# A two-layer encoder trunk on one Trainium2 core: the second layer starts with another product, and its first activations are made one half of the tokens at a time

## The chip, the cores and the metric

The kernel runs on one core of a Trainium2 chip. The metric is device time in microseconds (us) for the whole program, two layers from input to output. The engines are named as in the profile: PE (matrix multiplies; PEld is its weight load), DVE (vector), ACT (scalar), POOL (GpSimd), SP (which only issues transfers here). Each engine takes its instructions from a queue of its own in the order in which the program was built, and waits on semaphores for the others.

## What is computed

Two equal layers over 256 tokens of 2048 channels. Of a layer, cut to what matters here:

```python
h = rms_norm(x, norm_pre) * (1 + scale) + shift          # per-channel scale and shift
proj = h @ w_in                                          # all input products share h
rq, rk, rv, rg, lx, lg, mq, mkv, mkr, mg, merge_logits = split(proj)
y_ret, y_lru, y_mla = retention(rq, rk, rv, rg), rglru(lx, lg), mla(mq, mkv, mkr, mg)
merged = sum of sigmoid(merge_logits[b]) * (y_b @ w_branch[b])  over the three branches
y = merged @ w_out
x = x + (1 + res_gate) * rms_norm(y, norm_post)
```

The h of the second layer therefore needs the x of the first, and that needs the row sums of squares of y: two norms stand between the last product of layer one and the first product of layer two.

## The kernel before

**Tiles.** Tokens lie in two halves of 128 (hf 0 and 1), channels in 16 d-tiles of 128 (kt 0 to 15). Products are made in fp32r from split operands: a weight tile is cast to a high part `wh` on ACT (L308) and the rest `wl` is subtracted on DVE (L309), 128x1024 each; the activations are kept as pairs of a high and a low part in the same way. Each product is high*high + high*low + low*high, so three matmuls per step.

**Three forms of product.** `gemm_x` (L349) has the tokens as the stationary operand: a step is one d-tile and one half of the tokens, six matmuls of 512 columns. `gemm_w` (L377) has the weights stationary and 256 tokens moving: 384 matmuls of 256 columns for a product of 1024 output columns. `gemm_pair` (L396) also has the weights stationary, but moves high and low part in one matmul of 512 columns and adds one of 256: 128 of each. `run` (L978) chooses: lx, lg, mg, rq and rk are of the second kind, and they go through `gemm_pair` unless something has to be called between their steps (`before`), in which case they go through `gemm_w`.

**The end of layer one.** The last part of the product with `w_out` (L1190 to L1193) is sorted by half, so the bank of half 0 is complete some 5 us before that of half 1. Then the closing chain (L1205 to L1256), whose order on ACT, DVE and POOL is written out by hand: `close(hf)` squares the last quarter of y on ACT, weighs it on DVE (L1188) and makes 1/rms(y); `add(hf, k)` makes a quarter of the new x (L1224; one quarter, `ASIDE`, on POOL in L1221 and L1222); `sq` squares it on ACT (L477); `bias` and `rstd` make 1/rms(x).

**The start of layer two.** `h_chain` (L1068) multiplies x by 1/rms for both halves (L600, L603), then `h_tiles` (L605) turns the d-tiles on PE (L614, into a small PSUM bank `mi`), applies scale and shift (L617, DVE) and splits the result (L625 on ACT, L626 on DVE). The first three calls make d-tiles 0, 1 and 2 to 3; the others make two d-tiles each, ahead of the product that uses them. `hold` keeps the second half of the first weight load behind those first calls. The order of the products is `first` (L994): lx, lg, mqkv (the latents of the attention branch), mg and two merge logits. Since lx must call `h_chain` between its steps, it goes through `gemm_w`.

**What sets the order.** PE and SP run in the order in which the code is written. On the other engines a scheduler places instructions by priority; what is written by hand, or under `tc.high_priority(offset=LATE)`, stands ahead of the rest. Between ACT and DVE the framework lets only one at a time read a PSUM tile: an instruction that reads it waits until the other engine's read is over.

Of the kernel before, what the change touches and what calls it, by code (L numbers as in the profile page):

```python
# [19 lines left out]
P = 128  # L20
# [11 lines left out]
ASIDE = [((0, 3),), ((0, 3), (1, 0))]  # L32
# [22 lines left out]
def hybrid_trunk(ctx: ExitStack, tc: tile.TileContext, a, out):  # L55
# [293 lines left out]
    def gemm_x(act, w, r0, c0, kts, banks, ncol=W1, before=None, late=False):  # L349
# [3 lines left out]
        parts = [[k] for k in range(kts[0], kts[1], step)]  # L353
        if late:
            parts[-2:] = [parts[-2] + parts[-1]]
        for part in parts:
            steps, spare = [], []
            for k0 in part:
                nk = min(step, kts[1] - k0)
                if before is not None:  # L360
                    before(k0)
                pieces = load_split(wsrc(w, r0, k0, nk, c0, ncol), nk, ncol, spare if k0 > part[0] else None)
# [69 lines left out]
    def group(act, w, c0, mode, kts, res, func, partial, before):  # L432

        banks = [bank() for _ in range(4)]
        if mode == "x":
            drive(gemm_x(act, w, 0, c0, kts, [banks[0:2], banks[2:4]], before=before))
# [168 lines left out]
    def h_tiles(l, xs, act, k0, k1):  # L605
# [14 lines left out]
        return last  # L620

# [343 lines left out]
    def layer(l, xs, r):  # L965
        w_in = a["w_in"][l]
        H = Act(NKT)
# [10 lines left out]
        def run(n, kts=(0, NKT), partial=None, before=None):  # L978
# [7 lines left out]
            r = group(H, w_in, c0, m, kts, part.get(n), func, partial, before)  # L986
# [7 lines left out]
        first = ["lx", "lg", "mqkv", "mg", ("lru", 0), ("lru", 1)]  # L994
        lat = [None]
# [68 lines left out]
        else:  # L1064
            xn = [two() for _ in range(2)]
            done_k = [0]

            def h_chain():  # L1068
                with tc.high_priority(offset=LATE):
                    for c0 in (0, 2 * P):  # L1070
                        normed(xs, xn, r, c0, c0 + 2 * P, True)
                    for k in (0, 1):
                        h_tiles(l, xn, H, k, k + 1)
                    last = h_tiles(l, xn, H, 2, 4)
                hold.extend(last)
                for k in range(0, NKT, 2):
                    if k >= 4 and k % 4 == 0:
# [4 lines left out]
                    if k > 2:  # L1082
                        h_tiles(l, xn, H, k, k + 2)
# [5 lines left out]
            def ahead(k0):  # L1089
                while done_k[0] < min(NKT, k0 + 4):  # L1090
                    named["h"].step()

            for n in first:
                run(n, before=ahead if n == first[0] else None)
# [229 lines left out]
```

## Time and profile before

| | |
|---|---|
| median of 3 runs | 1984.01 us (1981.05 to 1984.06) |
| the profiled execution | 1987.14 us, of which the span from first to last instruction is 1985.4 us |
| PE busy | 1896.3 us, 96% of the span |
| DVE busy | 1427.9 us, 72% |
| ACT busy | 993.5 us, 50% |
| mean granted TensorE clock | 0.992 of full |

Matmuls are pipelined, so a busy PE is not PE at its peak: what tells is the distance from one start to the next and the time in which PE has nothing to do. The 40 slices of the page have PE at 9 tenths and over in all but four: the first, the third, the last, and the one from 993 to 1042 us, in which layer one ends.

### The profile page before, as it was taken

What the parts mean: (1) busy time and instruction counts of PE and PEld (TensorE: products, weight loads), DVE (VectorE), ACT (ScalarE), POOL (GpSimd) and SP (SyncE); (2) the same over time, 40 slices, a digit from 0 to 9 for tenths busy, and PEclk for the clock granted to TensorE, in tenths of its full rate; (3) what the DMA queues carried; (4) which work ended last, traced back from release to release, by engine and by line L of the source; (5) the groups of instructions that cost most, each with busy time, mean ns of one, the idle gap of its engine ahead of it and who ended that gap; (6) DMA issues with size and microseconds to landing.
All of it is one profiled execution on the core that took longest, in us unless ns stands there. A gap on an engine that the chain in (4) does not pass through costs nothing.

```text
span 1985.4 us, 25224 instructions
## 1 busy us (share of the span) xinstructions
PE 1896.3 (96%) x9884; PEld 1618.8 (82%) x9884; DVE 1427.9 (72%) x1832; ACT 993.5 (50%) x1301; POOL 187.4 (9%) x140
## 2 busy tenths in 40 slices
PE   1969999999999999999989999999999999999998
PEld 1868889778888888888879888888898888888786
DVE  7899989888877778877556765446575447886555
ACT  4744547834444445444454775444445444544443
POOL 2233411100000010101110010000000001010110
PEclk9989999999999999999999999999999999999999
DMA  8778774587877678878665555555554556878663
GB/s 261 281 270 297 270 260 154 203 282 269 264 257 271 236 275 271 279 286 279 214 219 185 170 170 191 197 195 179 184 189 149 200 196 219 271 274 285 219 213 127
DMA packets 169335, 457.06 MB, mean 230 GB/s; under 512 B 12224, under 2 KB 20432, under 8 KB 169216
## 3 DMA queue, kind: packets, MB, share of 16 engines
q1 hardware_dynamic: 165536, 443.44, 65.1%
q0 software_dynamic: 3536, 11.75, 1.9%
q8 instruction: 77, 1.26, 0.2%
q14 instruction: 42, 0.34, 0.0%
q10 hardware_dynamic: 144, 0.26, 0.0%
HBM read 451.23 MB, written 4.19 MB: 229 GB/s over the span
## 4 chain that ended last, share of the span: by engine, by line
PE 80%; DVE 11%; DMA 4%; ACT 2%; issue 2%; POOL 0%; DVEq 0%; ACTq 0%; POOLq 0%
PE acc L373 54%; PE acc L405 8%; DVE wl L309 4%; PE acc L406 4%; DVE slot L512 3%; PE acc L392 2%; PE acc L393 2%; PE acc L391 2%; DMA raw<-in_w_in 1%; DVE slot L446 1%; ACT wh L308 1%; DMA raw<-in_w_branch 1%; DMA raw<-in_mla_w_ukv 1%; DMA raw<-in_ada_w 1%; PE mi L858 1%
## 5 line engine op out<-in xcount | busy, mean ns | idle before, releaser
L309 DVE TENSOR_TENSOR wl<-raw,wh 128x1024 fp32r<-128x1024 f32 (+1 forms) x636 | 796.5, 1255 | 452.8 <-ACT wh L308 450.4
L308 ACT CAST wh<-raw 128x1024 fp32r<-128x1024 f32 (+1 forms) x636 | 662.4, 1045 | 790.9 <-PE acc L373 493.4
L373 PE MATMUL acc<-wh,pair 128*128 128x512 f32 x3552 | 990.7, 393 | 4.2 <-DVE slot L446 3.8
L373 PEld LDWEIGHTS acc<-wh,pair 128*128 128x128 f32 x3552 | 661.7, 188 | 145.1 <-DVE slot L446 7.3
L373 PE MATMUL acc<-wl,pair 128*128 128x512 f32 x1776 | 558.6, 391 | 6.6 <-DVE wl L309 6.6
L373 PEld LDWEIGHTS acc<-wl,pair 128*128 128x128 f32 x1776 | 332.5, 188 | 80.7 <-DVE wl L309 11.2
L405 PE MATMUL acc<-pair,wh 128*128 128x512 f32 x768 | 273.3, 400 | 1.0 <-DVE slot L419 1.0
L512 DVE SCALAR_TENSOR_TENSOR slot<-raw,c_act,slot 128x512 f32<-128x512 f32 (+1 forms) x326 | 255.8, 786 | 6.1 <-DMA raw<-in_ada_w 1.7
L406 PE MATMUL acc<-pair,wl 128*128 128x256 f32 x768 | 215.9, 281 | 1.8 <-DVE wl L309 1.7
L405 PEld LDWEIGHTS acc<-pair,wh 128*128 128x128 f32 x768 | 144.3, 188 | 35.8 <-DVE slot L419 1.3
L391 PE MATMUL acc<-pair,wh 128*128 128x256 f32 x512 | 148.9, 291 | 5.0 <-ACT pair L625 5.0
L392 PE MATMUL acc<-pair,wh 128*128 128x256 f32 x512 | 147.8, 289 | 0.8 <-DVE pair L626 0.8
L393 PE MATMUL acc<-pair,wl 128*128 128x256 f32 x512 | 147.8, 289 | 0.3 <-DVE wl L309 0.3
L406 PEld LDWEIGHTS acc<-pair,wl 128*128 128x128 f32 x768 | 145.1, 189 | 2.9 <-DVE wl L309 2.7
L391 PEld LDWEIGHTS acc<-pair,wh 128*128 128x128 f32 x512 | 101.2, 198 | 6.1 <-ACT pair L625 5.8
L392 PEld LDWEIGHTS acc<-pair,wh 128*128 128x128 f32 x512 | 101.1, 197 | 1.7 <-DVE pair L626 1.4
L393 PEld LDWEIGHTS acc<-pair,wl 128*128 128x128 f32 x512 | 100.9, 197 | 0.8 <-DVE wl L309 0.7
L507 POOL TENSOR_TENSOR slot<-slot,slot 128x512 f32<-128x512 f32 (+1 forms) x49 | 76.0, 1552 | 106.3 <-ACT slot L503 101.1
L1113 POOL TENSOR_TENSOR slot<-slot,slot 128x512 f32<-128x512 f32 x32 | 50.7, 1599 | 252.4 <-DVE slot L1110 252.4
L446 DVE TENSOR_TENSOR slot<-acc,slot 128x512 f32<-128x512 f32 x96 | 62.4, 680 | 2.3 <-PE acc L393 1.4
L850 POOL DMA_DIRECT2D slot<-in_ret_gn x4 | 2.3, 569 | 593.0 <-PE mi L802 362.6
L503 ACT ACTIVATE slot<-raw,c_act 128x512 f32<-128x512 f32 (+1 forms) x64 | 40.0, 662 | 28.3 <-DMA raw<-in_ada_w 28.0
(241 smaller groups left out, 1373.5 us busy)
## 6 DMA issues: line engine op xcount, KB each, us to landing
raw<-in_w_in SPq DMA_DIRECT2D x224, 1024.0 KB, 5.0
raw<-in_ada_w SPq DMA_DIRECT2D x96, 1024.0 KB, 6.7
raw<-in_w_branch SPq DMA_DIRECT2D x48, 1024.0 KB, 6.3
raw<-in_w_out SPq DMA_DIRECT2D x32, 1024.0 KB, 5.4
raw<-in_mla_w_ukv SPq DMA_DIRECT2D x8, 1024.0 KB, 5.9
raw<-in_mla_w_uq SPq DMA_DIRECT2D x8, 768.0 KB, 4.5
slot<-in_x SPq DMA_DIRECT2D x8, 512.0 KB, 8.8
slot<-in_k_decay POOLq DMA_DIRECT2D x4, 512.0 KB, 5.1
```

Source lines behind the costliest of these rows:

```text
L308: nc.scalar.copy(wh, raw[:, c0:c0 + n])
L309: sub = nc.vector.tensor_tensor(out=wl, in0=raw[:, c0:c0 + n], in1=wh.bitcast(F32), op=ALU.subtract)
L373: mm(b[:, 0:w_n], x, ws[:, j * w_n:(j + 1) * w_n], start=st, stop=sp)
L391: mm(dst, wh[:, cs], act.H(kt), start=first, stop=False, skip_group_check=True)
L392: mm(dst, wh[:, cs], act.L(kt), start=False, stop=False, skip_group_check=True)
L393: mm(dst, wl[:, cs], act.H(kt), start=False, stop=last, skip_group_check=True)
L405: mm(v3(b, T), wh[:, cs], act.both(kt), start=kt == 0, stop=False)
L406: mm(b[:, 0:T], wl[:, cs], act.H(kt), start=False, stop=kt == NKT - 1)
L446: nc.vector.tensor_tensor(out=dst, in0=b, in1=dst, op=ALU.add)
L507: nc.gpsimd.tensor_tensor(out=acc[1], in0=acc[1], in1=t, op=ALU.add)
L512: nc.vector.scalar_tensor_tensor(acc[0], src, c, acc[0], ALU.mult, ALU.add)
L1113: nc.gpsimd.tensor_tensor(out=dst, in0=dst, in1=gate[hf][:, cs], op=ALU.add)
```

## The change

1. **Order.** In layer two the order of the products starts with mqkv, then lx and lg. mqkv goes through `gemm_x` and now calls the h chain between its steps; lx goes through `gemm_pair`.
2. **First steps of mqkv.** `gemm_x` takes an argument `soon`. With it the first weight load (d-tiles 0 and 1) and a second one of half the size (d-tile 2) form one part, sorted by half: three steps of half 0, then three of half 1. `soon()` is called ahead of the first step of half 1 and ahead of the second. A load of d-tile 3 alone follows, then pairs as before.
3. **First d-tiles by halves.** A new function `h_half` makes d-tiles 0 to 3 of one half: four transposes into one bank, then for each d-tile one ACT instruction that applies scale and shift and casts to the high part, one DVE instruction that applies scale and shift in full precision, and for each two d-tiles one subtraction.
4. **Closing chain.** In layer one it is ordered by half: all of half 0 up to its 1/rms and the scaled first 512 columns (`begin`), then `close(1)`, one quarter of half 1, `h_half` of half 0, the other three quarters of half 1, and its 1/rms. No quarter goes to POOL. In layer two (the last) nothing moves.

```diff
-ASIDE = [((0, 3),), ((0, 3), (1, 0))]
+ASIDE = [(), ((0, 3), (1, 0))]
...
-        parts = [[k] for k in range(kts[0], kts[1], step)]
+        parts = [[(k, min(step, kts[1] - k))] for k in range(kts[0], kts[1], step)]
+        if soon is not None:
+            parts[:2] = [[(0, 2), (2, 1)], [(3, 1)]]
...
-            if part is parts[-1]:
+            opening = soon is not None and part is parts[0]
+            if part is parts[-1] or opening:
                 steps.sort(key=lambda s: s[1])
-            for kt, hf, (wh, wl) in steps:
+            for i, (kt, hf, (wh, wl)) in enumerate(steps):
+                if opening and i in (3, 4):
+                    soon()
...
+    def h_half(l, xn, act, hf):
+        b, t = mbank(), half_slot()
+        for k in range(4):
+            nc.tensor.transpose(b[:, k * P:(k + 1) * P], xn[hf][0][:, k * P:(k + 1) * P], ident)
+        h, lo = [v3(p, T)[:, :, hf * P:(hf + 1) * P] for p in act.piece(0)]
+        for k in range(4):
+            ks, g, s = slice(k * P, (k + 1) * P), gvec[l][:, k:k + 1], svec[l][:, k:k + 1]
+            i0 = nc.scalar.activation(out=h[:, k, :], in_=b[:, ks], func=AF.Identity, scale=g, bias=s)
+            nc.vector.tensor_scalar(t[:, ks], b[:, ks], g, s, ALU.mult, ALU.add)
+            if k % 2:
+                i1 = nc.vector.tensor_tensor(out=lo[:, k - 1:k + 1, :], in0=v3(t, P)[:, k - 1:k + 1, :], in1=h[:, k - 1:k + 1, :].bitcast(F32), op=ALU.subtract)
...
+        if l:
+            first[:3] = ["mqkv", "lx", "lg"]
...
+                    last = h_half(l, xn, H, 1)
+                yield 1
+                for k in range(4, NKT, 2):
...
+                for k in range(4):
+                    add(0, k)
+                    sq(0, k)
+                bias(0)
+                rstd(0)
+                begin(0)
+                close(1)
+                add(1, 0)
+                sq(1, 0)
+                hold.extend(h_half(l + 1, xn, Hn, 0))
+                for k in (1, 2, 3):
+                    add(1, k)
+                    sq(1, k)
+                bias(1)
+                rstd(1)
+                begin(1)
```

What the built programs show at three places follows; `_NNNN` numbers single tiles, `xss_1248` holds the sums of squares of half 1, `xss_1247` those of half 0, `mi` is the small PSUM bank, `pair_102` holds the first d-tiles of h, slots 79 and 82 hold the new x of half 1, slots 90 and 96 that of half 0 and half 1 times 1/rms, and what a row waits for stands in brackets.

ACT before, from the square root of half 0, behind the first square of half 1, to the first scaled columns of d-tiles 4 and up (L602):

```order
L458 ACTIVATE rstd_1259_8475<-xss_1247_8440,mean_8459 128x1
L477 ACTIVATE junk_8478,xss_1248_8441<-slot_79 128x512 [waits DVE_49,Activation_49]
L477 ACTIVATE junk_8481,xss_1248_8441<-slot_82 128x512 [waits DVE_49,Activation_49]
L477 ACTIVATE junk_8486,xss_1248_8441<-slot_82 128x512 [waits DVE_49,Activation_49]
L458 ACTIVATE rstd_1264_8488<-xss_1248_8441,mean_8483 128x1 [waits DVE_49,Activation_49]
L625 CAST pair_102<-slot_86 128x256 [waits DVE_49]
L625 CAST pair_102<-slot_87 128x256 [waits DMASW1_49,DVE_49]
L625 CAST pair_102<-slot_85 128x512 [waits DVE_49]
L308 CAST wh_8533<-raw_8527 128x1024
L308 CAST wh_8598<-raw_8596 128x1024 [waits DMAHW6_49]
L308 CAST wh_8602<-raw_8596 128x1024 [waits PE_49]
L602 ACTIVATE slot_90<-slot_81,rstd_1259_8475 128x512
```

Both square roots of x and the three casts of h come ahead of any weight cast. ACT now, from behind the same square to the scaled columns (L607):

```order
L635 ACTIVATE pair_102<-mi_8476,svec_136,gvec_135 128x128 [waits PE_49]
L635 ACTIVATE pair_102<-mi_8476,svec_136,gvec_135 128x128 [waits DVE_49] x3
L308 CAST wh_8524<-raw_8518 128x1024
L308 CAST wh_8530<-raw_8528 128x1024 [waits DMAHW6_49]
L482 ACTIVATE junk_8492,xss_1248_8441<-slot_79 128x512 [waits DVE_49,Activation_49]
L482 ACTIVATE junk_8495,xss_1248_8441<-slot_82 128x512 [waits DVE_49,Activation_49]
L482 ACTIVATE junk_8498,xss_1248_8441<-slot_82 128x512 [waits DVE_49,Activation_49]
L463 ACTIVATE rstd_1265_8503<-xss_1248_8441,mean_8500 128x1 [waits DVE_49,Activation_49]
L635 ACTIVATE pair_102<-mi_8552,svec_136,gvec_135 128x128 [waits PE_49]
L635 ACTIVATE pair_102<-mi_8552,svec_136,gvec_135 128x128 [waits DVE_49] x3
L308 CAST wh_8607<-raw_8605 128x1024 [waits DMAHW7_49,PE_49]
L607 ACTIVATE slot_90<-slot_81,rstd_1256_8463 128x512
```

Two weight casts (`wh_8524` and `wh_8530`, d-tiles 1 and 2) have moved in between the first square of half 1 and its other three, and the cast for d-tile 3 (`wh_8607`), which waits for PE, stands ahead of the scaled columns of d-tiles 4 to 7.

DVE before, from the reciprocal of half 1 to the first subtraction for a weight tile after it:

```order
L459 RECIPROCAL rstd_1264_8488<-rstd_1264_8488 128x1 [waits Activation_49]
L603 TENSOR_SCALAR slot_96<-slot_79,rstd_1264_8488 128x256 [waits DVE_49]
L603 TENSOR_SCALAR slot_96<-slot_79,rstd_1264_8488 128x256
L617 TENSOR_SCALAR slot_86<-mi_8506,gvec_135,svec_136 128x256 [waits PE_49,Pool_49]
L617 TENSOR_SCALAR slot_87<-mi_8512,gvec_135,svec_136 128x256 [waits PE_49]
L626 TENSOR_TENSOR pair_102<-slot_86,pair_102 128x256 [waits Activation_49]
L617 TENSOR_SCALAR slot_85<-mi_8518,gvec_135,svec_136 128x256 [waits PE_49,Pool_49]
L626 TENSOR_TENSOR pair_102<-slot_87,pair_102 128x256 [waits Activation_49]
L617 TENSOR_SCALAR slot_85<-mi_8518,gvec_135,svec_136 128x256
L626 TENSOR_TENSOR pair_102<-slot_85,pair_102 128x512 [waits Activation_49]
L603 TENSOR_SCALAR slot_96<-slot_79,rstd_1264_8488 128x512
L309 TENSOR_TENSOR wl_8534<-raw_8527,wh_8533 128x1024 [waits Activation_49]
```

Ahead of these rows the quarters of half 1, its mean and its reciprocal follow each other with no weight tile among them. DVE now, from the last instructions of the first d-tiles of half 0 to the multiplication that starts half 1:

```order
L636 TENSOR_SCALAR slot_86<-mi_8476,gvec_135,svec_136 128x128 [waits Activation_49] x2
L638 TENSOR_TENSOR pair_102<-slot_86,pair_102 128x2x128 [waits DVE_49]
L1242 SCALAR_TENSOR_TENSOR slot_79<-slot_79,rstd_1258_8470,slot_91 128x512
L1242 SCALAR_TENSOR_TENSOR slot_82<-slot_82,rstd_1258_8470,slot_94 128x512 x2
L309 TENSOR_TENSOR wl_8525<-raw_8518,wh_8524 128x1024 [waits Activation_49]
L470 TENSOR_REDUCE mean_8500<-xss_1248_8441 128x1 [waits Activation_49]
L309 TENSOR_TENSOR wl_8531<-raw_8528,wh_8530 128x1024 [waits DMAHW6_49]
L471 TENSOR_SCALAR mean_8500<-mean_8500 128x1 [waits DVE_49]
L464 RECIPROCAL rstd_1265_8503<-rstd_1265_8503 128x1 [waits Activation_49]
L1257 TENSOR_SCALAR slot_96<-slot_79,rstd_1265_8503 128x512 [waits DVE_49]
```

Two weight subtractions (L309) now stand between the quarters of half 1 and its reciprocal, and the three later quarters stand behind the whole of `h_half` of half 0.

PE before, from the end of the product with `w_out` to the first matmuls of lx:

```order
L373 MATMUL acc_8305<-pair_103,pair_101 128x512 x6
L614 MATMUL mi_8506<-ident,slot_90 128x128
L614 MATMUL mi_8506<-ident,slot_96 128x128
L614 MATMUL mi_8512<-ident,slot_90 128x128
L614 MATMUL mi_8512<-ident,slot_96 128x128
L614 MATMUL mi_8518<-ident,slot_90 128x128
L614 MATMUL mi_8518<-ident,slot_96 128x128
L614 MATMUL mi_8518<-ident,slot_90 128x128
L614 MATMUL mi_8518<-ident,slot_96 128x128
L391 MATMUL acc_8498<-pair_102,wh_8529 128x256
L392 MATMUL acc_8498<-pair_102,wh_8529 128x256
L393 MATMUL acc_8498<-pair_102,wl_8530 128x256
```

All transposes of d-tiles 0 to 3, both halves, stand ahead of the first matmul. PE now, behind the 18 matmuls of half 0, from the transposes of half 1 to those of d-tiles 4 and 5:

```order
L631 MATMUL mi_8552<-ident,slot_96 128x128 x4
L378 MATMUL acc_8516<-wh_8520,pair_102 128x512
L378 MATMUL acc_8517<-wh_8520,pair_102 128x512
L378 MATMUL acc_8516<-wl_8521,pair_102 128x512
L378 MATMUL acc_8517<-wl_8521,pair_102 128x512
L378 MATMUL acc_8516<-wh_8520,pair_102 128x512
L378 MATMUL acc_8517<-wh_8520,pair_102 128x512
L619 MATMUL mi_8575<-ident,slot_90 128x128
L619 MATMUL mi_8575<-ident,slot_96 128x128
L619 MATMUL mi_8575<-ident,slot_90 128x128
L619 MATMUL mi_8575<-ident,slot_96 128x128
```

One step of half 1 (six matmuls) stands between the two sets of transposes, and all the rest of half 1 stands behind the second set.

## Rows read from the trace of the kernel before

**Rows 1.** PE's waits from 1047 us to the end, all there are.

```profile
PE acc L373 <- DVE wl L309: 0.8, 1, 0.8
```

**Rows 2.** Timeline around the end of layer one: start, us, instructions [idle before <-releaser].

```profile
1030.31 2.51 DVE L1224 SCALAR_TENSOR_TENSOR slot<-slot,rstd,slot 128x512 f32<-128x512 f32 x3
...
1031.10 0.63 ACT L477 ACTIVATE junk<-slot 128x512 f32<-128x512 f32 x1 [1.29 <-DVE slot L1224]
...
1031.31 2.88 PE L373 MATMUL acc<-pair,pair 128*128 128x512 f32 x12
...
1034.29 0.60 ACT L477 ACTIVATE junk<-acc 128x512 f32<-128x512 f32 x1 [0.56 <-PE acc L373]
...
1035.88 2.08 DVE L1224 SCALAR_TENSOR_TENSOR slot<-slot,rstd,slot 128x512 f32<-128x512 f32 x3
...
1036.72 0.63 ACT L477 ACTIVATE junk<-slot 128x512 f32<-128x512 f32 x1 [0.80 <-DVE slot L1224]
```

**Rows 3.** The same timeline, from the second root of x to the first matmuls.

```profile
1039.03 0.63 ACT L477 ACTIVATE junk<-slot 128x512 f32<-128x512 f32 x1
...
1039.79 0.29 ACT L458 ACTIVATE rstd<-xss,mean 128x1 f32<-128x1 f32 x1
...
1040.11 0.16 DVE L459 RECIPROCAL rstd<-rstd 128x1 f32<-128x1 f32 x1 [0.66 <-ACT rstd L458]
...
1040.31 0.62 DVE L603 TENSOR_SCALAR slot<-slot,rstd 128x256 f32<-128x256 f32 x2
...
1042.67 0.56 PE L391 MATMUL acc<-pair,wh 128*128 128x256 f32 x1
```

**Rows 4.** Stretches: length, busy us (instructions) of PE, PEld, DVE, ACT, POOL, clock, DMA share, GB/s.

```profile
1036.00:1038.00 2.00, 0.00 (x0) 0.00 (x0) 2.00 (x5) 1.27 (x4) 0.41 (x1) 0.66 0.94 270
...
1046.00:1047.00 1.00, 1.00 (x8) 1.00 (x7) 1.00 (x2) 1.00 (x2) 0.00 (x0) 0.56 0.00 0
1047.00:1048.00 1.00, 1.00 (x11) 1.00 (x10) 1.00 (x2) 0.46 (x2) 0.00 (x0) 1.00 0.00 0
```

**Rows 5.** PE timeline: starts of matmuls in `gemm_w` and `gemm_pair`, and of four transposes.

```profile
1046.66 0.38 PE L391 MATMUL acc<-pair,wh 128*128 128x256 f32 x1
1046.87 0.28 PE L392 MATMUL acc<-pair,wh 128*128 128x256 f32 x1
...
1048.31 0.28 PE L392 MATMUL acc<-pair,wh 128*128 128x256 f32 x1
...
1050.35 0.60 PE L614 MATMUL mi<-ident,slot 128*128 128x128 f32 x4
...
1093.25 0.40 PE L405 MATMUL acc<-pair,wh 128*128 128x512 f32 x1
...
1109.86 0.40 PE L405 MATMUL acc<-pair,wh 128*128 128x512 f32 x1
```

**Rows 6.** PE timeline: starts of matmuls in `gemm_x`, three in 0.68 us.

```profile
1020.21 0.62 PE L373 MATMUL acc<-wh,pair 128*128 128x512 f32 x2
...
1020.89 0.62 PE L373 MATMUL acc<-wh,pair 128*128 128x512 f32 x2
```

**Rows 7.** By line: durations ns min/median/max, first and last start us, forms.

```profile
L887 ACT ACTIVATE slot<-mi,bnm,brs x32: 448/457/467, 744.9 to 1738.6; 128x128 f32<-128x128 f32 x32
L693 ACT COPY krs<-mi x2: 254/256/257, 380.2 to 1336.9; 128x128 f32<-128x128 f32 x2
L617 DVE TENSOR_SCALAR slot<-mi,gvec,svec x32: 533/541/547, 40.8 to 1083.6; 128x256 f32<-128x256 f32 x32
L694 DVE TENSOR_TENSOR krs<-mi,krs x2: 283/284/285, 387.9 to 1338.2; 128x128 f32<-128x128 f32 x2
```

**Rows 8.** Timeline: weight casts, subtractions and the scaled columns of d-tiles 4 to 15.

```profile
1045.02 1.99 ACT L308 CAST wh<-raw 128x1024 fp32r<-128x1024 f32 x2
1046.15 3.70 DVE L309 TENSOR_TENSOR wl<-raw,wh 128x1024 fp32r<-128x1024 f32 x3
1048.50 1.95 ACT L602 ACTIVATE slot<-slot,rstd 128x512 f32<-128x512 f32 x3
```

More of the change, by code (lines that the diff above doesn't have):

```diff
@@ L357, in gemm_x @@
             steps, spare = [], []
-            for k0 in part:
-                nk = min(step, kts[1] - k0)
+            for k0, nk in part:
                 if before is not None:
                     before(k0)
-                pieces = load_split(wsrc(w, r0, k0, nk, c0, ncol), nk, ncol, spare if k0 > part[0] else None)
+                pieces = load_split(wsrc(w, r0, k0, nk, c0, ncol), nk, ncol, spare if late and k0 > part[0][0] else None)
                 for k in range(nk):
@@ L430, in act_slice, with group @@
         return res[i // 2][:, (i % 2) * 512:(i % 2 + 1) * 512]
-    def group(act, w, c0, mode, kts, res, func, partial, before):
+    def group(act, w, c0, mode, kts, res, func, partial, before, soon=None):
         banks = [bank() for _ in range(4)]
         if mode == "x":
-            drive(gemm_x(act, w, 0, c0, kts, [banks[0:2], banks[2:4]], before=before))
+            drive(gemm_x(act, w, 0, c0, kts, [banks[0:2], banks[2:4]], before=before, soon=soon))
         else:
@@ L985, in run @@
                 return
-            r = group(H, w_in, c0, m, kts, part.get(n), func, partial, before)
+            r = group(H, w_in, c0, m, kts, part.get(n), func, partial, before, soon)
             if partial in (None, "last"):
@@ L1064, in layer @@
         else:
-            xn = [two() for _ in range(2)]
-            done_k = [0]
+            done_k = [4]
             def h_chain():
                 with tc.high_priority(offset=LATE):
[L1070 to L1077, printed above, removed]
+                    last = h_half(l, xn, H, 1)
+                yield 1
+                for k in range(4, NKT, 2):
+                    if k % 4 == 0:
                         with ExitStack() as order:
@@ L1089, in ahead @@
             def ahead(k0):
-                while done_k[0] < min(NKT, k0 + 4):
+                while k0 >= 4 and done_k[0] < min(NKT, k0 + 4):
                     named["h"].step()
             for n in first:
-                run(n, before=ahead if n == first[0] else None)
+                run(n, before=ahead if n == first[0] else None, soon=named["h"].step if n == first[0] else None)
                 if n == first[0]:
@@ L1205, in layer @@
         with tc.manual_schedule(engines={ENG.Activation, ENG.DVE, ENG.Pool}), tc.high_priority(offset=LATE):
+            Hn, xn = None, None
+            if l < DEPTH - 1:
+                Hn, xn = Act(NKT), [two() for _ in range(2)]
             ry, xbias, xss = [None, None], [None, None], [small([P, 4], "xss4", 2) for _ in range(2)]
@@ L1236, in rstd, with begin @@
                     rx.append(rstd_of(xss[hf][:, 3:4], 1, D, xbias[hf]))
+            def begin(hf):
+                nc.vector.tensor_scalar(xn[hf][0][:, 0:512], yA[hf][0][:, 0:512], rx[hf], None, ALU.mult)
             close(0)
-            for k in (3, 0, 1, 2):
-                add(0, k)
-            for k in range(3):
-                sq(0, k)
-            bias(0)
-            close(1)
-            sq(0, 3)
-            add(1, 0)
-            add(1, 1)
-            sq(1, 0)
-            add(1, 2)
-            rstd(0)
-            sq(1, 1)
-            add(1, 3)
-            sq(1, 2)
-            bias(1)
-            sq(1, 3)
-            rstd(1)
+            if l < DEPTH - 1:
+                for k in range(4):
[14 more added lines that the diff above has]
+                begin(1)
+            else:
+                for k in (3, 0, 1, 2):
+                    add(0, k)
+                close(1)
+                for k in range(4):
+                    add(1, k)
             if l < DEPTH - 1:
```

18 lines of the change are left out of this document (9 added, 9 removed).

## The prediction

> **What bounds the kernel now.** I read the share of busy time first, then PE's list of waits. Behind 1047 us PE waits once, for 0.8 us [rows 1], so layer two is paid in matmuls, and the only idle time that the change can buy back is the opening of that layer. The timeline of that opening shows it: the last matmul of `w_out` ends at 1031.31 + 2.88 = 1034.19 [rows 2], and the first matmul of lx starts at 1042.67 [rows 3], 8.48 us later. In between runs one chain: square of y, 1/rms, three quarters of the new x on DVE in 2.08 us, squares 0.75 apart on ACT, root at 1039.79, reciprocal, scaled columns at 1040.31, transposes [rows 2, 3]. The stretches show a second price: granted clock 0.66 in 1036 to 1038, when PE had nothing to do, still 0.56 in 1046 to 1047, and 1.00 after that [rows 4]. A matmul of 256 columns starts 0.21 us after its neighbour just before 1046.87 and 1.44 / 12 = 0.12 us behind it [rows 5]; these are the levels 1.2 and 2.4 GHz. The 4.2 us from 1042.67 to 1046.87 thus hold 1.9 us that the full clock would have saved. Opening plus clock is 10.4 us; the change aims at that.
>
> **The products, outside the opening.** All is set against the profiled execution, 1987.14 us (3.1 above the median of 1984.01, of which the same may be added or taken). A step of four transposes adds 0.67 us (1050.35 to the matmul after the next) less two matmuls, taken as 0.47 a set with its wait [rows 5]. Before: lx through `gemm_w` is 384 x 0.12 = 46.1; with 8.48, 1.9 and 6 sets (2.8) that is 59.3, and the trace has lg's first matmul at 1093.25, so 59.06 after 1034.19 [rows 5]. A pair in `gemm_pair` takes (1109.86 - 1093.25) / 47 = 0.353, so 128 are 45.2 [rows 5]; `gemm_x` has three matmuls in 0.68, 0.2267 each, so 192 are 43.5 [rows 6]. The three products from 1034.19 take 59.06 + 45.2 + 43.5 = 147.8 now. After the change they take what mqkv takes with its opening, and 2 x 45.2. Exchanging 46.1 for 45.2 alone would be a gain of 0.9; everything else hangs on when PE has worked off the opening of mqkv.
>
> **Half 0.** Its first quarter starts at 1030.31 as now; the fourth no longer goes to POOL, and DVE makes it in about 0.69 (2.08 / 3) [rows 2]. POOL's share vanishes and costs DVE 0.7 us, hidden, since `close(1)` can't start before 1034.29. Squares start at 1031.10 [rows 2], 0.75 apart, so they end near 1034.1; mean, root and reciprocal take 0.5 (1039.79 to 1040.31 is such a piece [rows 3]), the scaled 512 columns 0.5, four transposes 0.6: PSUM holds half 0 at 1035.8. ACT and DVE, though, come there late: `close(1)` and the first quarter of half 1 stand ahead of `h_half`, at the times of now, so ACT is free at 1036.72 + 0.7 = 1037.4 [rows 2].
>
> `h_half` reads one bank from both engines, and every read waits for the other engine's. The trace has no such pair at 128x128 with scale and shift. ACT's nearest row is 0.457 (the same form, L887), its least 0.254 (a plain copy); DVE's are 0.541 (the same operation at 256 columns) and 0.283 (128 columns, another operation) [rows 7]. I take 0.457, since form and size are equal, and 0.41, the middle, plus 0.03 at each hand-over, as between root and reciprocal (1039.79 + 0.29 to 1040.11 [rows 3]): 0.92 a d-tile, between 0.59 and 1.07. Four take 3.7: ACT is through at 1040.6, DVE with its last subtraction at 1041.4. The first matmul can start at 1037.9, 4.8 us earlier than now; that is the gain.
>
> **What it costs.** Behind `h_half` ACT has, by the order of the built program, the casts of d-tiles 1 and 2, 1.0 each [rows 8], up to 1042.5, and only then three squares of half 1, which now end at 1039.66 [rows 3]. DVE makes the three quarters from 1041.4 to 1043.4 and then, still ahead of the reciprocal, two weight subtractions of 1.23 [rows 8], up to 1046.0. With mean, root, reciprocal and scaled columns, half 1 is ready for its transposes at 1047.0; now its reciprocal is done at 1040.3. PE meanwhile has d-tile 0 of half 0 (done at 1040.2), two matmuls of d-tile 1 at 1041.5, and a wait for the first subtraction up to 1044.7: some 3 us. With PE idle from 1034.19, as now, and then working in pieces, I take the clock to be at 1.2 GHz here; the remaining ten matmuls start 0.43 apart (twice the 0.21 [rows 5]), up to 1048.95, transposes up to 1050.05. Then the turn-taking again: first matmul of half 1 at 1050.55, its low part at 1052.35, d-tile 0 done at 1053.0. The cast of d-tile 3 waits for that on ACT, and queued behind it are the scaled columns of d-tiles 4 to 7 (L607, 1.95 / 3 = 0.65 [rows 8]): 1053.2 + 1.05 + 0.65 gives transposes at 1054.9, a new stall of 2 us, which PE cannot pass, since its queue has the rest of half 1 behind those transposes. The load of d-tile 2 is wanted at 1041.5. DMA share is 0.94 in 1036 to 1038 and 0.00 in 1046 to 1048 [rows 4], so it lands in time or lengthens the 3 us wait; I take nothing.
>
> At 1054.9 PE has done 24 of 192 matmuls. The other 168 x 0.2267 = 38.1 and 6 x 0.47 = 2.8 end at 1095.8, 61.6 us after 1034.19. Sum: 61.6 + 45.2 + 45.2 = 152.0 against 147.8, **+4.2 us**. Put otherwise, 20.7 us go by from 1034.19 to 1054.9 for 5.4 us of work, 15.3 lost where 10.4 are lost now. The ends of the turn-taking move this: 0.59 a d-tile, twice four of them, gives +1.3 with the clock down; 1.07 gives +6.9 (1.2 us more in the two halves, and 1.5 for the matmuls that slip back into the low clock).
>
> **Rivals.** *The clock stays at 2.4 GHz.* The transposes at 1035.2 and the matmuls from 1037.9 break the idle time that now runs to 1039. Then ten matmuls cost 0.2267 instead of 0.43 and transposes half, 2.4 us less: +1.8, 1985.8 on the median's scale. Against it: the clock of now stayed low through the transposes and rose 4.2 us after dense matmuls began [rows 3 to 5], and dense work here starts no earlier than 1044.7. The Trainium skill ("TensorE: Matmul & The Clock Gate", "What's actually happening") says that the throttled state is the default and that activity releases it; by that sentence the early matmuls could hold the clock. Its section "Part 4: PE-mode transpose" says that transposes do not count as busy in that way, which speaks against the half of this rival that rests on them; the low clock through the transposes of now agrees with it. Chance 0.18.
>
> *Not slower: short turns.* If a pair of reads takes 0.59 (the copy and the 128-column rows of [rows 7]), `h_half` is through 1.3 us earlier per half and the casts, quarters and subtractions move up with it: +1.3, or -0.1 if the clock also holds. 1983.9 to 1985.3, middle 1984.6. It decides below some 0.65 a d-tile. Against it stands L887, equal in form, at 0.457. Chance 0.11; a real gain beyond -4 us would need both stalls gone as well, chance 0.03.
>
> *Worse: the clock falls again or rises late.* PE stops at 1053.0 for 2 us. If the low level covers d-tile 0 of half 1 (6 x 0.2 = 1.2) and 4.2 us of dense work behind 1054.9 (2.0 lost), that is +7.4, 1991.4. Chance 0.08.
>
> **How the numbers follow.** The forecast, +4.2 on the median, is **1988.2 us**, chance 0.60, its own range +3 to +6. 0.2% or 4.0 us is what a measurement can tell from no change. The forecast lies on that line: of its 0.60 I put 0.38 above it and 0.22 below. Same: 0.22 + 0.18 (clock) + 0.08 (short turns) = 0.48. Slower: 0.38 + 0.08 = 0.46. Faster: 0.03 + 0.03 = 0.06. The range runs from the middle of the short turns, 1984.2 with a little for the runs' spread, to the late clock, 1991.4.
>
> **What the trace after would show.** The first matmul 3.7 us behind the last of `w_out` instead of 8.5; ACT's L635 at 0.457 and DVE's L636 at 0.41 in strict turns; a wait of PE for DVE's `wl` (L309) near 3 us, and one of the transposes L619 for ACT's L607 near 2; half 1's scaled columns 12 to 13 us behind 1034.19; clock low through the 18 matmuls of half 0; lx's first matmul 61.6 us behind the end of `w_out`. I am wrong if PE's wait for `wl` is short because the weight work does not stand in half 1's way, if the clock is 1.00 in 1040 to 1050, or if something outside the three products moves.

## The result

The changed kernel takes 1992.80 us (median of 6 runs, 1992.05 to 1994.67) against 1983.68 us of the kernel before (6 runs). By the medians it is slower by 9.1 us; the ratio of the means is 1.0051, 95% interval 1.0038 to 1.0064. The forecast was +4.2, 1988.2, with a range up to 1991.4: the sign was right, the size forecast less than half of what came.

The profiled execution of the changed kernel took 1992.05 us, with a span of 1990.3. Layer one differs from execution to execution by some us (in the profiles of this document it ends between 1030.48 and 1036.99), so places in layer two are told here by their distance from the end of `w_out`, as in the prediction. In the changed kernel that end is at 1030.00 + 2.88 = 1032.88.

PE's timeline of its opening (start, us, instructions, idle before and its releaser), which answers to [rows 2, 3]:

```profile
1030.00 2.88 PE L378 MATMUL acc<-pair,pair 128*128 128x512 f32 x12
1033.97 0.63 PE L631 MATMUL mi<-ident,slot 128*128 128x128 f32 x4 [1.08 <-DVE slot L1257]
1036.48 1.22 PE L378 MATMUL acc<-wh,pair 128*128 128x512 f32 x2 [1.89 <-ACT pair L635]
...
1040.30 1.22 PE L378 MATMUL acc<-wh,pair 128*128 128x512 f32 x2 [0.69 <-ACT wh L308]
1043.40 1.22 PE L378 MATMUL acc<-wl,pair 128*128 128x512 f32 x2 [1.88 <-DVE mean L470]
...
1047.13 0.60 PE L631 MATMUL mi<-ident,slot 128*128 128x128 f32 x4
...
1052.66 0.73 PE L619 MATMUL mi<-ident,slot 128*128 128x128 f32 x4 [1.79 <-ACT slot L607]
1053.07 1.17 PE L378 MATMUL acc<-wh,pair 128*128 128x512 f32 x2
...
1057.51 0.60 PE L619 MATMUL mi<-ident,slot 128*128 128x128 f32 x4
...
1095.27 0.39 PE L410 MATMUL acc<-pair,wh 128*128 128x512 f32 x1
```

The first matmul comes 3.60 us behind `w_out` in place of 8.48, and then PE is held up again and again: by the turns of ACT and DVE, by the cast and the subtraction of d-tile 1 (the matmul at 1043.40 reads `wl`; the small mean beside it ended later by the profile), and by the scaled columns of d-tiles 4 to 7. The same stretch on ACT and DVE, single rows:

```profile
1036.98 0.46 ACT L635 ACTIVATE pair<-mi,svec,gvec 128x128 fp32r<-128x128 f32 x1 [0.55 <-DVE slot L636]
1037.47 0.41 DVE L636 TENSOR_SCALAR slot<-mi,gvec,svec 128x128 f32<-128x128 f32 x1 [0.53 <-ACT pair L635]
1037.92 0.46 ACT L635 ACTIVATE pair<-mi,svec,gvec 128x128 fp32r<-128x128 f32 x1 [0.48 <-DVE slot L636]
...
1039.22 1.98 ACT L308 CAST wh<-raw 128x1024 fp32r<-128x1024 f32 x2
1042.13 1.22 DVE L309 TENSOR_TENSOR wl<-raw,wh 128x1024 fp32r<-128x1024 f32 x1
1045.23 0.49 DVE L1257 TENSOR_SCALAR slot<-slot,rstd 128x512 f32<-128x512 f32 x1
...
1050.95 1.03 ACT L308 CAST wh<-raw 128x1024 fp32r<-128x1024 f32 x1
1051.88 1.95 ACT L607 ACTIVATE slot<-slot,rstd 128x512 f32<-128x512 f32 x3
```

Strict turns, 0.94 us a d-tile; two weight casts behind them; half 1's scaled columns at 1045.23. The granted clock (last column but two) by stretches:

```profile
1036.00:1038.00 2.00, 1.52 (x4) 1.17 (x4) 0.90 (x3) 0.97 (x4) 0.00 (x0) 0.51 0.51 182
...
1044.00:1046.00 2.00, 2.00 (x6) 1.61 (x5) 1.26 (x4) 0.29 (x1) 0.00 (x0) 0.50 1.09 248
1046.00:1048.00 2.00, 1.74 (x9) 1.17 (x8) 0.00 (x0) 0.23 (x1) 0.00 (x0) 0.93 0.87 262
1052.00:1054.00 2.00, 1.34 (x6) 1.20 (x7) 1.99 (x4) 1.83 (x3) 0.00 (x0) 0.78 0.77 299
1054.00:1056.00 2.00, 2.00 (x6) 1.57 (x5) 1.88 (x5) 0.64 (x2) 0.00 (x0) 0.50 0.70 188
```

It is at 1.2 GHz from 1036 to 1046 and again from 1053 to 1056.5. Behind the opening, all places of PE's timeline from 1060 us to the end at which it waits over 0.3 us, where [rows 1] had one of 0.8:

```profile
1219.16 1.13 PE L948 MATMUL mi<-slot,slot 128*128 128x256 f32 x4 [0.80 <-ACT slot L951]
1220.84 1.13 PE L948 MATMUL mi<-slot,slot 128*128 128x256 f32 x4 [0.54 <-ACT slot L951]
1241.32 0.80 PE L378 MATMUL acc<-wh,pair 128*128 128x512 f32 x2 [1.33 <-DVE slot L424]
```

These 2.67 us lie beside and behind mg, 160 us after the opening. The gates of the LRU branch (L948) stand there in PE's queue, beside a product of the kind that empties four banks in its middle. ACT has those evictions, a silu (L426) and the gates' sigmoids (L951) to do at once, and each change between silu and sigmoid has a table load of 1.28 us; the four sigmoids of one set of gates are torn apart, and PE's next gates wait for them:

```profile
1212.24 1.28 ACT L951 ACT_TABLE_LOAD   x1
1213.54 0.47 ACT L951 ACTIVATE slot<-mi,vec 128x256 f32<-128x256 f32 x1
1214.03 1.28 ACT L426 ACT_TABLE_LOAD   x1
1215.33 1.06 ACT L426 ACTIVATE slot<-slot 128x1024 f32<-128x1024 f32 x1
1216.29 1.03 ACT L308 CAST wh<-raw 128x1024 fp32r<-128x1024 f32 x1
1217.34 1.28 ACT L951 ACT_TABLE_LOAD   x1
...
1239.48 0.91 ACT L423 COPY slot<-acc 128x256 f32<-128x256 f32 x3
1240.76 1.41 DVE L424 TENSOR_TENSOR slot<-acc,slot 128x256 f32<-128x256 f32 x4
```

The last two rows are the evictions at the end of mg, behind a weight cast and a weight subtraction in their queues; the product behind mg waits for them, 1.33 us. In the kernel before the same gates (L928 at 1163.21 and 1170.39) lay beside mqkv, which empties no bank before its end. ACT made four sigmoids in a row there, and PE waited for none of them:

```profile
1165.76 1.57 ACT L931 ACTIVATE slot<-mi,vec 128x256 f32<-128x256 f32 x4
```

### The profile page after: what moved, and what is told of

Its sections match the earlier page's. It is cut to its first block, busy times and chain, and to the rows that moved or that the text cites. A ratio compares the mean times of both kernels' runs of the same rounds, so it can differ in the third digit from the quotient of the medians.

```text
span 1990.3 us, 24996 instructions
## 1 busy us (share of the span) xinstructions
PE 1899.4 (95%) x9756; PEld 1612.5 (81%) x9756; DVE 1431.7 (72%) x1844; ACT 999.0 (50%) x1312; POOL 180.7 (9%) x138
## 4 chain that ended last, share of the span: by engine, by line
PE 81%; DVE 11%; ACT 3%; DMA 2%; issue 2%; POOL 0%; DVEq 0%; ACTq 0%; POOLq 0%
PE acc L378 57%; PE acc L410 9%; PE acc L411 5%; DVE wl L309 4%; DVE slot L517 3%; DVE slot L451 1%; PE acc L397 1%; PE acc L398 1%; PE acc L396 1%; ACT wh L308 1%; DMA raw<-in_mla_w_ukv 1%; DMA raw<-in_ada_w 1%; PE mi L878 1%; PE mi L796 0%; PE mi L797 0%
## 5 line engine op out<-in xcount | busy, mean ns | idle before, releaser
L309 DVE TENSOR_TENSOR wl<-raw,wh 128x1024 fp32r<-128x1024 f32 (+1 forms) x636 | 794.6, 1252 | 457.6 <-ACT wh L308 455.3
L308 ACT CAST wh<-raw 128x1024 fp32r<-128x1024 f32 (+1 forms) x636 | 663.0, 1045 | 799.0 <-PE acc L378 526.6
L410 PE MATMUL acc<-pair,wh 128*128 128x512 f32 x896 | 317.3, 398 | 1.0 <-DVE slot L424 1.0
L410 PEld LDWEIGHTS acc<-pair,wh 128*128 128x128 f32 x896 | 168.2, 188 | 40.9 <-DVE slot L424 1.3
L396 PE MATMUL acc<-pair,wh 128*128 128x256 f32 x384 | 110.6, 288 | 4.9 <-ACT pair L645 4.9
L397 PE MATMUL acc<-pair,wh 128*128 128x256 f32 x384 | 110.4, 287 | 0.8 <-DVE pair L646 0.8
L396 PEld LDWEIGHTS acc<-pair,wh 128*128 128x128 f32 x384 | 75.1, 196 | 6.0 <-ACT pair L645 5.7
L397 PEld LDWEIGHTS acc<-pair,wh 128*128 128x128 f32 x384 | 75.1, 196 | 1.7 <-DVE pair L646 1.4
L533 PE MATMUL mi<-ident,slot 128*128 128x128 f32 x64 | 10.4, 303 | 45.2 <-DVE slot L521 45.2
```

The costliest lines, as they stand in the source:

```text
L308: nc.scalar.copy(wh, raw[:, c0:c0 + n])
L309: sub = nc.vector.tensor_tensor(out=wl, in0=raw[:, c0:c0 + n], in1=wh.bitcast(F32), op=ALU.subtract)
L396: mm(dst, wh[:, cs], act.H(kt), start=first, stop=False, skip_group_check=True)
L397: mm(dst, wh[:, cs], act.L(kt), start=False, stop=False, skip_group_check=True)
L410: mm(v3(b, T), wh[:, cs], act.both(kt), start=kt == 0, stop=False)
```

## The experiments

Medians are of the timed runs of each kernel; the kernel before gave 1983.94, 1984.82 and 1984.66 us beside the three sets. The changed kernel was timed only with the result above (1983.68 beside it), so a difference of medians to it can be off by about 1 us. The other columns are read from PE's timeline of each profile, as distances from the end of `w_out`: the transposes of half 1, the first matmul of lx (where mqkv ends), and the first transpose of the rotary key `krs`, which follows the same products in all. One profile stands for each kernel.

| kernel | median us | half 1 transposed | lx starts | krs |
|---|---|---|---|---|
| before, first profile | 1984.01 | | | 301.72 |
| e1 before again | 1984.27 | | | 301.92 |
| changed kernel | 1992.80 | 14.25 | 62.39 | 309.50 |
| e2 order only | 1985.99 | | 56.62 | 303.69 |
| e3 mg later | 1988.17 | 14.94 | 61.92 | 306.26 |
| e4 weights early | 1989.80 | 12.49 | 59.07 | 306.44 |
| e5 scaled first | 1989.74 | 15.08 | 61.03 | 308.44 |
| e6 two banks | 1986.50 | 12.84 | 57.01 | 304.38 |
| e7 70 fillers | 1995.05 | 18.18 | 65.84 | 313.21 |
| e8 three edits | 1982.81 | 11.71 | 55.89 | 300.23 |
| e9 33 fillers | 1989.59 | 12.97 | 59.52 | 306.61 |
| e10 e8 and POOL | 1982.62 | 11.85 | 56.02 | 300.37 |
| e11 e8 and fillers | 1983.52 | 11.42 | 55.56 | 299.91 |
| e12 e8 and both | 1983.20 | 11.72 | 55.91 | 300.26 |

**e1, the kernel before once more.** 

> The kernel before once more, to see how far one execution differs from the next. Its first profile took 1987.14 us, 3.1 above the median of its timed runs, and had the last matmul of w_out end at 1034.19 us. If layer one alone makes these differences (transfers at the start), that landmark moves by 1 to 3 us in the new profile, while the stretch from it to the first matmul of lg stays at 59.1 us within 0.3. If instead layer two wobbles, that stretch differs by a us or more.

The end of `w_out` came at 1032.23 in place of 1034.19, and krs 0.2 us from where it was relative to it. Of the 2.9 us between the two spans 2.0 lie ahead of that end and 1.1 behind krs, so a distance from one to the other is good to some tenths. In the opening of the changed kernel it is less good: e3 below has the same opening and starts lx 0.5 us earlier. By krs the changed kernel loses 309.50 - 301.72 = 7.8 us, which lies within the interval of the result (7.5 to 12.7 us).

**e2, the order alone.** The kernel before with this edit only:

```diff
+        if l:
+            first[:3] = ["mqkv", "lx", "lg"]
```

> The kernel before with the first part of the change alone: mqkv, lx, lg in layer two, mqkv through gemm_x with the h chain between its steps, lx through gemm_pair; closing chain and first d-tiles as before. Theory O (the order by itself costs): the chain of the LRU branch, which runs beside the products behind lg, now lies beside mg, a gemm_pair product, and PE waits some 2.7 us behind it as in the profile after; the opening is that of before (8.5 us without a matmul), the three products take 0.9 us less, sum about +2, 1985.5 to 1986. Rival: the waits behind lg come from the late opening and not from the order; then -0.7 to -0.9, 1983, and no wait of PE for the gates of the LRU branch.

Ratio 1.0010, interval 1.0001 to 1.0018; in the trace +2.0 at krs. The waits are there, with the opening of before:

```profile
1035.38 0.44 PE L614 MATMUL mi<-ident,slot 128*128 128x128 f32 x1 [4.89 <-DVE slot L600]
...
1210.98 1.13 PE L928 MATMUL mi<-slot,slot 128*128 128x256 f32 x4 [0.79 <-ACT slot L931]
1212.65 1.13 PE L928 MATMUL mi<-slot,slot 128*128 128x256 f32 x4 [0.54 <-ACT slot L931]
...
1233.13 0.80 PE L373 MATMUL acc<-wh,pair 128*128 128x512 f32 x2 [1.32 <-DVE slot L419]
```

So 2.0 of the 7.8 us come from the order, 5.8 from the halves: lx starts at 56.62 here and at 62.39 in the changed kernel.

**e3, mg later.** The changed kernel with one line changed:

```diff
-            first[:3] = ["mqkv", "lx", "lg"]
+            first[:5] = ["mqkv", "lx", "lg", ("lru", 0), "mg"]
```

> The changed kernel with one swap behind lg: the first merge logits of the LRU branch ahead of mg, so that the LRU chain lies beside a gemm_x product again. Theory O: the waits of PE for the LRU gates (1.3 us in two) and for an eviction behind mg (1.3 us) go away and the time falls by 2 to 2.7 us against the changed kernel, about 1990. Rival (the waits come from something else in the opening): they stay, 1992 to 1993.

Behind 1060 us PE waits for nothing any more. From the start of lx to krs it takes 244.34 us in place of 247.11, so the edit is worth 2.8 us; 3.2 less at krs and 4.6 in the medians hold the 0.5 us of the opening and the difference between sets as well. With e2 that is the cause of the waits, taken away and put in by itself.

This run shows something else. Its opening is that of the changed kernel, with the same stall of 1.79 us, but the clock behaves otherwise: the first low stretch lasts past 1048, beyond the transposes of half 1 (14.94), and there is no second one behind the stall (two rows of PE's timeline, then the stretch between them):

```profile
1053.35 0.66 PE L619 MATMUL mi<-ident,slot 128*128 128x128 f32 x4 [1.79 <-ACT slot L607]
...
1056.59 0.60 PE L619 MATMUL mi<-ident,slot 128*128 128x128 f32 x4
...
1054.00:1056.00 2.00, 2.00 (x11) 1.64 (x10) 2.00 (x6) 1.38 (x3) 0.00 (x0) 1.00 0.40 47
```

**e4, weights early.** The first weight load's second half is held behind the square root of half 1's y and no longer behind `h_half`; that pulls d-tile 2 along:

```diff
-                close(1)
+                hold.append(close(1))
...
-                hold.extend(h_half(l + 1, xn, Hn, 0))
+                h_half(l + 1, xn, Hn, 0)
```

> The changed kernel with the weight casts of d-tiles 1 and 2 placed right behind the closing of half 1's y on ACT, ahead of its squares, and their subtractions ahead of the first d-tiles of half 0 on DVE. Theory W (weight work between the quarters of half 1 and its 1/rms starves PE): PE's wait of 1.9 us inside d-tile 1 goes, half 1's scaled columns come about 1 us earlier, and the matmuls of half 0 run dense from about 4.5 us behind the end of w_out; the transposes of d-tiles 4 and 5 come 1.5 to 3 us earlier and the time falls by as much, 1990 to 1991. Rival (the turn-taking sets the pace, weight work has room): the first d-tiles of half 0 come 1 us later and all is as late as now, 1992.5.

3.1 us less at krs, 3.0 in the medians. The gap of 1.88 us inside d-tile 1 is gone: its low-weight matmuls follow the high ones, and the clock rises inside half 0's matmuls.

```profile
1040.48 2.08 PE L378 MATMUL acc<-wh,pair 128*128 128x512 f32 x4 [0.39 <-DVE pair L638]
1042.35 1.06 PE L378 MATMUL acc<-wl,pair 128*128 128x512 f32 x2
1043.20 1.59 PE L378 MATMUL acc<-wh,pair 128*128 128x512 f32 x4
...
1046.48 0.63 PE L631 MATMUL mi<-ident,slot 128*128 128x128 f32 x4 [0.76 <-DVE slot L1260]
```

Half 0 now waits longer for its first d-tiles (2.31 us in place of 1.89), as the rival had it, but that cost less than the starved step. The stall of 1.79 us ahead of d-tiles 4 and 5 is still there, and as in e3 the clock does not fall behind it; so about half of the 3.1 us may be the clock's share in the one profile of the changed kernel, though lx starts 2.9 us earlier than in e3 too.

**e5, scaled columns first.** In `h_chain` of the changed kernel:

```diff
                 with tc.high_priority(offset=LATE):
+                    normed(xs, xn, r, 4 * P, 8 * P)
                     last = h_half(l, xn, H, 1)
...
-                    if k % 4 == 0:
+                    if k % 4 == 0 and k > 4:
```

> The changed kernel with the scaled columns of d-tiles 4 to 7 (one ACT, one DVE instruction) ahead of the first d-tiles of half 1, in time in which both engines wait for PE. Theory: PE's wait of 1.8 us in front of the transposes of d-tiles 4 and 5 comes from ACT's queue (cast of d-tile 3, then the scaled columns) and goes away; since PE no longer stops there, the second fall of the clock behind it goes too. 1.8 us at least and 3.5 to 4 with the clock, 1989 to 1991. Rival (PE then waits for the low weights of d-tile 3 or for d-tiles 4 and 5 a few steps on): under 0.5 us, 1992.5.

The stall of 1.79 us is gone, and the clock stays at 1.00 from 1048 to 1058; but in e3, with the stall, it is 1.00 from 1050 on as well. e3, which transposes half 1 as late (14.94), is the nearer comparison: the transposes of d-tiles 4 and 5 come 19.09 us behind `w_out` in place of 20.91, those of 6 and 7 22.29 in place of 24.15. The next ones give back a part of the 1.8 us, since DVE's scaled columns of d-tiles 8 and up are now late:

```profile
1050.00 0.60 PE L619 MATMUL mi<-ident,slot 128*128 128x128 f32 x4
...
1057.43 0.55 PE L619 MATMUL mi<-ident,slot 128*128 128x128 f32 x3 [0.76 <-DVE slot L608]
```

0.9 us are left at lx against e3, 1.1 at krs against the changed kernel; the medians say 3.1, from five runs between 1989.6 and 1992.7. The rival was right by the trace in that the wait moved on, if not all of it.

**e6, two banks.** Transposes of d-tiles 0, 1 and 2, 3 of a half in separate banks; ACT works through 0, 1, 2, 3 and DVE through 2, 3, 0, 1:

```diff
-        b, t = mbank(), half_slot()
+        bs, t = (mbank(), mbank()), half_slot()
...
-        for k in range(4):
+        for ka, kd in ((0, 2), (1, 3), (2, 0), (3, 1)):
```

> The changed kernel with the four transposes of a half in two PSUM banks; ACT starts with the first, DVE with the second, then they swap, so that they no longer wait for each other at each d-tile. The same instructions otherwise, though the scheduler now puts the first scaled columns of d-tiles 4 to 7 ahead of the cast of d-tile 3 as well. Theory T (turn-taking, 0.94 us a d-tile in the profile after): a half takes about 2 us on ACT in place of 3.3 and 2.4 on DVE in place of 3.7; half 1 starts 1.3 us earlier, its own d-tiles 1.2 us earlier, and the stall of 1.8 us goes; 3.5 to 5 us with the clock, 1988 to 1989. Rival (weight work behind the first d-tiles takes up what becomes free, or the transposes pay for it): only the stall's share, 1990 to 1991.

5.1 us less at krs, 6.3 in the medians: the largest single effect. It is not the turns' alone. As its expectation says, the first scaled columns now stand ahead of the cast of d-tile 3 (L607 at 1046.74, the cast at 1047.97), so the stall that e5 removed is gone here too; and the granted clock, 0.88 in 1036 to 1038 and 1.00 before, fell some 5.7 us behind `w_out` in this profile, 3.2 in that of the changed kernel, so half 0's first step ran at 2.4 GHz; how the 5.1 us divide among the three is not shown. Half 0 takes 1.49 us on ACT:

```profile
1034.16 0.73 DVE L635 TENSOR_SCALAR slot<-mi,gvec,svec 128x128 f32<-128x128 f32 x2
1034.90 1.49 ACT L634 ACTIVATE pair<-mi,svec,gvec 128x128 fp32r<-128x128 f32 x4
1035.72 0.73 DVE L635 TENSOR_SCALAR slot<-mi,gvec,svec 128x128 f32<-128x128 f32 x2 [0.84 <-ACT pair L634]
...
1047.73 0.71 PE L619 MATMUL mi<-ident,slot 128*128 128x128 f32 x4
```

Back to back an instruction takes 0.37 us, against 0.47 for one half of a turn. The Trainium skill ("PSUM — Partial Sum Buffer", "PSUM bank collisions raise a hardware error") names it an error when two engines touch one bank in the same partitions at the same time, reads against reads included, so the turns could not simply be dropped in one bank. Another bank is the way round it: here the two engines read at the same time from 1035.72 on.

**e7, fillers.** Products of the identity with itself on PE in the gaps of the opening:

```diff
+    def fill(n):
+        for _ in range(n):
+            nc.tensor.matmul(fbank[0][:, 0:P], ident, ident, start=True, stop=True)
...
+        if hf == 0:
+            fill(16)
...
+                    if i == 4:
+                        fill(14)
                     soon()
...
+                if opening and i == 1:
+                    fill(14)
...
+                    if opening and i == 1 and x is xh and ws is wh:
+                        fill(26)
```

> The changed kernel with 70 small matmuls of the identity into a bank that nobody reads, put on PE into its four gaps of the opening (16 behind the transposes of half 0, 14 and 26 around d-tile 1, 14 ahead of the transposes of d-tiles 4 and 5), to price the clock. At full clock one takes some 0.1 us, so they fit the gaps. Theory C (the low clock costs the opening 4 to 5 us in its two stretches): the granted clock stays at 1.00 throughout, the waits for ACT and DVE grow by part of what is saved, and 2 to 3.5 us are left, 1989 to 1991. Rival (ACT and DVE set the pace, the low clock lies beside their work): the clock is high and the transposes of half 1 come no earlier, under 1 us, 1992 to 1993.

It gives no price for the clock. One filler takes 0.22 us, not 0.1 (two records each), so the third set, of 26, ran on from 1046.10 to 1051.8, while half 1's scaled columns had been there since 1048.8:

```profile
1046.10 5.97 PE L637 MATMUL mi<-ident 128*128 128x128 f32 x52
```

The clock, though, was 1.00 throughout.

**e9, fewer fillers.** The same calls with other numbers, into a bank of the finished product:

```diff
-            fill(16)
+            fill(8)
...
-                        fill(14)
+                        fill(8)
...
-                    fill(14)
+                    fill(6)
...
-                        fill(26)
+                        fill(11)
```

> The changed kernel with fillers again, now fewer: 33 multiplications of the identity into an old bank (8 behind the transposes of half 0, 6 and 11 around d-tile 1, 8 ahead of the transposes of d-tiles 4 and 5), 0.22 us each as measured in the first try, which filled the gaps beyond their end. If the clock is the price, it stays at 1.00 and the 18 matmuls of half 0 no longer lie at 1.2 GHz; the transposes of half 1 come at 1045.7 in the scale of the profile after (bound by half 1's scaled columns) in place of 1047.1, the matmuls behind 1052.7 lose no second stretch (2.4 us): 3 to 4 us in sum, 1989 to 1990. If ACT and DVE set the pace throughout, under 1.5 us.

Clock 1.00 in every stretch from 1032 to 1056, 2.9 us less at krs, 3.2 in the medians:

```profile
1036.00:1040.00 4.00, 3.28 (x23) 2.79 (x22) 3.25 (x7) 3.04 (x6) 0.21 (x1) 1.00 0.02 5
1040.00:1044.00 4.00, 4.00 (x28) 3.57 (x28) 3.54 (x8) 2.18 (x7) 1.78 (x3) 1.00 0.77 262
1044.00:1048.00 4.00, 2.81 (x13) 1.70 (x12) 1.98 (x5) 1.42 (x4) 0.00 (x0) 1.00 0.90 240
```

The fillers compute nothing, so this is the clock's share of the 5.8 us of the opening: 2.9 by lx against the changed kernel, 2.4 against e3, whose opening is the same.

**e8, three edits together.** The diffs of e3, e4 and e6 in one kernel. 

> The changed kernel with three of these edits together: the LRU logits ahead of mg, weight casts of d-tiles 1 and 2 early, two banks per half. If the causes add up (4.6 and 3.0 measured, 3 to 5 expected of the banks, less what two of them share), the time is 1981 to 1984, the first time level with or below the kernel before. If they all release the same wait, it stays at 1986 to 1988.

1982.81 us; ratio to the kernel before 0.9991, interval 0.9982 to 1.0000. The effects at krs add up to 9.3 us, of 11.4 for the three alone: the stall of e6 and the starved step of e4 share a part. PE's waits behind 1045 us to the end:

```profile
PE acc L378 <- DVE pair L638: 0.4, 1, 0.4
```

But lx starts at 55.89, only 0.7 earlier than in e2 with the opening of before. The clock still falls in it. The kernel before with e3's order and no halves was not run; the lx of e2 and the stretch from lx to krs of e3 give an estimate of 56.62 + 244.34 = 300.96 for its krs, 0.8 earlier than before. So about half of what e8 gains at krs (1.5 us) would come without any halves.

**e10 to e12, more on top of e8.** The first line in e10, the second in e11, both in e12:

```diff
-ASIDE = [(), ((0, 3), (1, 0))]
+ASIDE = [((1, 3),), ((0, 3), (1, 0))]
...
+        if hf == 0:
+            fill(8)
```

> The three edits together, and the last quarter of half 1's new x on POOL. DVE makes two quarters in place of three (0.7 us less) ahead of half 1's 1/rms; POOL's two instructions take 2 us from the reciprocal of y on and are done before the second square. Theory: half 1's scaled columns come 0.7 us earlier at most, and 0 to 0.7 us are left, 1982 to 1983. Rival (POOL beside DVE slows DVE, as three quarters took 2.51 us beside it and 2.08 without): no gain or 0.5 us more.

> The three edits together, and 8 fillers on PE (1.75 us) behind the transposes of half 0, in its gap of 2.3 us. If they hold the clock at 2.4 GHz, the 18 matmuls of half 0 take 4.1 us in place of 7.3, half 1's transposes are then bound by its scaled columns 0.9 us earlier than now: 0.9 us less, 1982. If the clock falls a little later all the same, nothing, 1982.8.

> All together: the three edits, a quarter on POOL, 8 fillers. If the low clock hid the gain of POOL's quarter (PE bound by half 0's matmuls) and the late half 1 hid that of the clock, both together bring more than their sum, 1.5 to 2 us below the three edits, 1981. If either is without effect, 1982 to 1983.

All three stand within 0.8 us of e8 in the medians and within 0.4 in the trace; neither edit is worth anything here. With the fillers of e11 the clock fell all the same, some 3 us later behind `w_out` than in e8:

```profile
1040.00:1042.00 2.00, 1.21 (x4) 0.98 (x5) 1.97 (x5) 0.17 (x1) 0.00 (x0) 0.79 0.89 328
1042.00:1044.00 2.00, 2.00 (x6) 1.59 (x5) 1.37 (x4) 1.94 (x6) 1.19 (x3) 0.50 1.03 397
```

e10 (0.9989, 0.9981 to 0.9998) and e12 (0.9988, 0.9979 to 0.9997) are faster than the kernel before by about 2 us, 0.1%, and so, most likely, is e8; a margin near the limit of what these runs tell.

## Why the prediction was too small

**Right, with its sizes.** The first matmul behind `w_out`: 3.7 us forecast, 3.60 measured. A turn of ACT and DVE: 0.92, and 0.94. Half 1's scaled columns 12 to 13 us behind `w_out`: 12.35. A new stall for L607 near 2 us: 1.79. The transposes of d-tiles 4 and 5 at 20.7: 19.78. The clock low through the matmuls of half 0, which the first rival denied: low from 1036 on. From the two first matmuls of d-tile 1 to the two that need `wl` it takes 3.10 us (1040.30 to 1043.40), 3.2 forecast; PE's idle part of it is 1.88 and not 3, since the sum left out the time of the two matmuls themselves. The chain of the opening was the right one, and e4, e6 and e5 took its links away one by one, e6 two of them together. With it the sign was no luck: the sum had lx 4.9 us later than its own terms give for the order alone (61.6 against 8.48 + 1.9 + 2.8 + 43.5 = 56.7), and measured are 5.8 (62.39 against 56.62), 5.3 by e3.

**A term that missed in one trace: the clock behind the stall.** The sum had 168 matmuls at full speed from the transposes of d-tiles 4 and 5 on. The clock fell a second time there, at 1053: twelve matmuls took from 1053.07 to 1057.51, 4.4 us where 2.7 were meant. That is the third rival's mechanism at its second place, with 1.7 us; it had 0.08 of the chances. lx started at 62.39, not 61.6: 1.7 more behind the stall, 0.9 less ahead of it, where the clock had risen before the transposes of half 1. But e3 and e4 have the same stall, and their twelve matmuls took 2.8 us with the clock at 1.00. In e3 the low clock lasted through the transposes of half 1, as the sum had it, and the transposes of d-tiles 4 and 5 came at 20.91 (forecast 20.7) and lx at 61.92 (forecast 61.6). So the opening was forecast within 0.3 to 0.8 us, and the second fall is a matter of the single execution; what decides it stays open.

**The step that failed: nothing behind the three products.** The sum ended with lg and took all else as it was. It counted the exchange of the products' forms (1.7; the same in the traces, from 244.34 us between the start of lx and krs in e3, where PE waits for nothing, against 242.66 between the start of lg and krs before), but did not ask what runs beside each product in its new place. The LRU chain starts behind lx, and its second gates come some 70 us behind the end of lx (1163.21 against 1093.25 before): beside mqkv before, beside mg after the change. That is 2.7 us of waits: the order alone starts lx early enough for a gain of 0.7 (56.62 + 2 x 45.2 against 147.8), and e2 measured a loss of 2.0. The end of the prediction named this case ("if something outside the three products moves") and gave it no price, nor a place in the range.

**The scale.** The sum was put on the median of before from an execution 3.1 us above it. The forecast's 4.2 with the 2.7 of the waits and the 0.8 of the opening makes 7.7; the traces compared from the end of `w_out` give 7.8, the medians 9.1. What the last 1.3 us are is not shown; against the medians of before beside the later sets the difference is 8.0 to 8.9.

## What to carry to other kernels

When products change their order, go through every chain that runs beside them and see which product each now lies against: evictions in the middle of a product, table loads and bank releases are paid there, far from the edit. Splitting a closing chain by halves starts PE early, but PE then lives on single steps; before it is worth anything, the weight work must be out of the second half's way and the two readers of PSUM in different banks, and even so it was worth 0.7 us here. And a stall that follows a short burst can cost clock as well as its length: of three profiles with the same stall of 1.79 us, one paid 1.7 us more behind it.

## What was not expected of the hardware

In the changed kernel the clock fell around 1053, though PE had been at work again since 1043.40 with gaps of 0.55, 0.66 and 1.79 us only and the granted clock was 1.00 from 1048 to 1052. In e3 the gaps were 0.55, 0.64 and 1.79 us and in e4 0.55, 0.65 and 1.79, and the clock behind them was 1.00. So the granted clock in one profile is no property of the kernel alone. Small products of the identity, which compute nothing, kept it at 1.00 through the same opening in e9, while eight of them in e11 only put the fall off by some 3 us against e8. The Trainium skill ("TensorE: Matmul & The Clock Gate", "What's actually happening") has activity release the throttle; e9 agrees. The Trainium skill ("TensorE: Matmul & The Clock Gate", "Part 4: PE-mode transpose") does not count transposes as such work; in the changed kernel four of them, 0.63 us at 1033.97, did not keep the clock from falling by 1036. That fits, but no run puts other work of the same length in their place.
